# Second half of the output gate computed in two groups of 512 columns, three pair-steps by sums, with the side work placed anew

## The chip, the cores and the metric

The kernel runs on one core of a Trainium2 chip. The metric is the device time of one execution in microseconds, as the median of several runs. A core has five engines that run side by side, each in the order of its own instructions: TensorE (PE, with its weight loads as PEld), VectorE (DVE), ScalarE (ACT), GpSimd (POOL) and SyncE (SP), which here issues most of the DMAs.

## The reference

One layer: a gated linear attention mixer and a squared-ReLU MLP, each with an RMS norm ahead and a residual around it, for 256 tokens of width 2048 in fp32. Only the lines that the change touches in some way:

```python
def _gla_mixer(h, w_in, w_gate_up, b_gate, o_norm, w_out):
    proj = h @ w_in
    q, k, v, r, g_low = jnp.split(proj, [...], axis=-1)      # widths 1024, 1024, 2048, 2048, 16
    ...                                                        # o: the chunked attention, 256 x 2048
    o = o * lax.rsqrt(jnp.mean(o * o, axis=-1, keepdims=True) + EPS) * o_norm
    return (o * jax.nn.silu(r)) @ w_out

h = x
h = h + _gla_mixer(_rmsnorm(h, gla_norm), w_in, w_gate_up, b_gate, o_norm, w_out)
h = h + _sq_relu_mlp(_rmsnorm(h, mlp_norm), w_up, w_down)
return _rmsnorm(h, final_norm)
```

The change is in how the second half of `r` (columns 1024 to 2047 of the gate) is computed, and in what is done beside it.

## The kernel before, in words

**Numbers.** fp32 values are split into a high and a low part of a type that TensorE takes at full rate. A product is three matmuls: high by high, low by high, high by low. Weights arrive by DMA in `raw` tiles (six in turn, with a seventh now and then); ACT casts the high part (`copy_hi`, L123) and DVE subtracts it from the raw tile for the low part (L136). There are five slots for high and low parts. Tokens are two tiles of 128; a matmul has 128 x 128 against 128 x 256.

**Two ways for a group of 512 columns.** `x_group` (L731) calls `group` (L294), which walks over eight pair-steps of 2 x 128 rows of `w_in` in a given order. A plain pair-step is 24 matmuls. A pair-step in the list `summed` is done by sums: the 2 x 2 blocks of weights and of activations are added up such that seven block products do the work of eight, which makes 21 matmuls. Nine of them go at once, on the plain blocks and a block that an accumulating DMA of POOL (L335) has added up; the other twelve are "pending" and stand behind the next step's matmuls, since DVE first has to form the sums of the weights (`weight_sums`, L233 and L234), ACT to cast them and DVE to subtract (L365). At the end of a group with summed steps, `combine` adds up the two banks of sums (ACT copies L735 and L736, DVE L737 to L740), and `put_all` adds the plain banks (L745) and hands each token tile on. For the gate that is `gate_x`: Silu on ACT (L803) and the product with the attention's output `on` on DVE (L804). The function in `between[step]` is run after that step. Four such groups, V0 and V1 for values and G0 and G1 for the gate's first half, precede the place of the change.

**The gate's second half.** It is computed by `natural` (L183): 16 steps of 128 rows and 24 matmuls (L181), over 1024 columns at a time, accumulated in four banks. Rows 5 and 6 (`EVEN`) are inserted at places 3 and 5. After each step `pump` takes functions from the deque `side` and from `jobs`. Behind the third step stand two turns, then four loads of the residual (`load_h`, 0.5 MB each, SP's queue), then `begin_out(0)`, which copies the residual into the banks of the output projection's first group. `jobs` holds two pieces of `make_sums` (L242), which form sums of `w_out` ahead of their use. At the end `gate_out` makes four Silu (L823) and four products with `on` (L824).

**Turns.** `turn(..., q)` transposes the columns of `on` for four blocks of 128 (eight PE transposes, L845) and splits them for use as activations of the output projection; for pair-rows 0, 1, 6 and 7 it forms their block sums too (L834 to L837), for the others it writes plain high and low parts (ACT L858, DVE L859). Turns 0 and 1 need columns 0 to 1023 of `on`, turns 2 and 3 the rest. Turns 2 and 3 stand behind the second step of the output projection's first group, `out_group(0)`, whose order begins with the pair-rows 3 and 0.

**What sets the order.** Each engine runs its instructions in the order of the program that a scheduler arranges, with `issue_after` tying certain casts, subtractions and matmuls to one another. PE is in order throughout: a transpose that waits holds all matmuls behind it.

Of the kernel before, what the change touches and what calls it, by code (L numbers as in the profile page):

```python
# [29 lines left out]
AF = mybir.ActivationFunctionType  # L30
# [17 lines left out]
G = 1024  # L48
# [21 lines left out]
def tile_gla_mlp(ctx, tc, x, xt, cols, w_vg, w_in, w_gate, w_out, w_up, w_down, final_norm, out):  # L70
# [657 lines left out]
        scores(hd)  # L728
        scores(hd + 1, spare)

    def x_group(n, c0, order, summed, between, put, rows_of={}):  # L731

        def combine(p16, p57):
            tt = nc.vector.tensor_tensor
            nc.scalar.copy(comb_x[:, 1::2], two(p16))  # L735
            nc.scalar.copy(comb_x[:, 0::2], two(p57))  # L736
            tt(comb_x[:, 3], comb_x[:, 1], comb_x[:, 3], op=ALU.add)  # L737
            tt(comb_x[:, 0], comb_x[:, 0], comb_x[:, 3], op=ALU.subtract)
            tt(comb_x[:, 3], comb_x[:, 3], comb_x[:, 2], op=ALU.add)
            tt(comb_x[:, 2], comb_x[:, 0], comb_x[:, 2], op=ALU.subtract)  # L740

        def put_all(banks):
            for t in range(NT):
                o = comb_x[:, 2 * t : 2 * t + 2]
                nc.vector.tensor_tensor(o, two(banks[t]), o, op=ALU.add)  # L745
                put(o.rearrange("p f s -> p (f s)"), t)

        def at_of(kp):
            def at(k):
                if k < A12:  # L750
                    return [x_forms[kp][:, i, k] for i in range(2)]
                t, i = divmod((A11, A12, A21, A22).index(k), 2)
                return plain_x(2 * kp + i, t)
            return at

        def row(kt, t):
            return (row_x if (kt, t) in [(2 * kp + i, t) for kp in rows_of for t, i in rows_of[kp][:1]] else plain_x)(kt, t)

        group(
            lambda kp: w_in[2 * kp * P : 2 * (kp + 1) * P, c0 : c0 + GT], [psum_bank(i) for i in x_banks[n % 2]], x_sums,  # L760
            order, summed, between, row, at_of, combine, put_all, filled=False, rows_of=rows_of,
        )

    V0 = (5, 6, 2, 0, 7, 3, 4, 1), (0, 4)
# [41 lines left out]

    x_group(2, 4 * KEYW, *G0, {i + 1: f for i, f in enumerate(attends[:6])}, gate_x(0), {2: FIRST[2]})
    x_group(3, 4 * KEYW + GT, *G1, {i: f for i, f in enumerate(attends[6:])}, gate_x(GT), {2: FIRST[2]})
    acc_free.clear()
    acc_free.extend(x_banks[0] + x_sums + x_banks[1])  # L810
    jobs.extend(next(make))


    oth = otl = None

    some = mid.tile([P, 7, 512], F32, tag="qt", name="some")

    def gate_out(acc, c0):
        for c in range(2):
            for t in range(NT):  # L820
                lo = c0 + 512 * c
                s = some[:, 2 * c + t]
                nc.scalar.activation(s, acc[t][c], AF.Silu, scale=r1[:, t : t + 1])  # L823
                nc.vector.tensor_tensor(on[:, t, lo : lo + 512], on[:, t, lo : lo + 512], s, op=ALU.mult)  # L824

    FORMED = (0, 1, 6, 7)
    raw_forms = [in_forms(some[:, 4:6].rearrange("p a b -> p (a b)")), in_forms(mid.tile([P, G], F32, tag="db", name="form"))]
# [11 lines left out]
    def turn(src, row, gain, q, forms_of=None, banks=None):  # L839

        bs = banks or [aux_bank(), aux_bank()]
        for i in range(4):
            kt, b, o = 4 * q + i, bs[i // 2], i % 2 * T
            for t in range(NT):
                newest[0] = nc.tensor.matmul(  # L845
                    b[:, o + t * P : o + (t + 1) * P], src[:, t, kt * P : (kt + 1) * P], ident, is_transpose=True,
                    start=i % 2 == t == 0, stop=i % 2 == t == 1, skip_group_check=True,
                ).ins
        for kp in (2 * q, 2 * q + 1):
            if forms_of and kp in FORMED:  # L850
                turn_pair(kp, bs[kp - 2 * q], gain, forms_of(kp))
                continue
            for kt in (2 * kp, 2 * kp + 1):
                i = kt - 4 * q
                b, o = bs[i // 2], i % 2 * T
                s = b[:, o : o + T].rearrange("p (t s) -> p t s", t=NT)
                dh, dl = row(kt)
                nc.scalar.activation(dh, s, AF.Copy, scale=gain(kt))  # L858
                nc.vector.scalar_tensor_tensor(dl, s, gain(kt), dh.bitcast(F32), op0=ALU.mult, op1=ALU.subtract)  # L859

    once_x = lambda kt, t: (plain_x if kt == EVEN[1] else row_x)(kt, t)
    oth, otl = (big.tile([P, KT * T + 192], F32R, tag="B", name="ot" + i) for i in "hl")

    of_pairs = big.tile([P, 4 * G + 64], F32R, tag="C", name="of")[:, OFF:-16].rearrange("p (b i f s) -> p b i f s", b=2, i=2, f=8)
# [37 lines left out]
    def spare_out(g):  # L902
        return [psum_bank(out_ids[2 * (1 - g % 2) + t], "aux") for t in range(NT)]

    side.extend([nothing] * 2 + [lambda: (
        turn(on, turned_o, gain_o, 0, forms_o),
        turn(on, turned_o, gain_o, 1, forms_o, [psum_bank(i, "aux") for i in r_banks[4:]]),
    )])
    side.extend([nothing] + [lambda i=i: load_h(i % 2, i // 2) for i in range(4)] + [nothing] * 2 + [lambda: begin_out(0)])
    r_banks = list(acc_free)  # L910
    out_ids = r_banks[4:] + r_banks[:4]
    acc = natural(once_x, rows(w_in, 5 * KEYW), G, HALF, order=even_at(3, 5))
    flush()
    gate_out(acc, G)
    hs = const.tile([P, NT, 4], F32, name="hs")

    GROUPS = D // GT
# [27 lines left out]
    def ssq_h(g):  # L945
# [5 lines left out]
    newest[0] = None  # L951
    ordered[0] = True
    out_group(0, ORDER[0], FORMED, {
        1: lambda: (turn(on, turned_o, gain_o, 2), turn(on, turned_o, gain_o, 3, forms_o, spare_out(0))),
        3: lambda: begin_out(1),
    })
    hth, htl = (big.tile([P, KT, T], F32R, tag="A" + i, name="h" + i, bufs=1) for i in "hl")
# [517 lines left out]
```

## Time and profile before

| | us |
|---|---|
| median of 3 runs | 1040.14 |
| lowest and highest | 1039.99, 1042.02 |
| span of the profiled execution | 1038.7 |
| PE busy in it | 1030.1 (99%) |
| DVE busy | 903.9 (87%) |
| ACT busy | 754.8 (73%) |
| POOL busy | 136.1 (13%) |
| gate's second half on PE (L181) | 238.41 to 283.76 |

The profiled execution's span lies 1.4 us under the median of the runs. Line numbers are those of the kernel before. A row of a timeline joins neighbouring instructions of one form; its time goes from the first start to the last end, so that pitches are read from one start to the next.

### The profile page before, as it was taken

The numbers are of one execution on the slowest core, as the hardware profiler recorded it, in microseconds if no ns is written. First come the engines' busy times: TensorE is split into PE (matmuls) and PEld (weight loads), VectorE is DVE, ScalarE is ACT, GpSimd is POOL, SyncE is SP. The second block draws the span as 40 slices with busy tenths as digits, with TensorE's granted clock in tenths as the row PEclk, the third lists the DMA queues.
The fourth block names the chain that finished last, engine by engine and source line by source line (L and its number), as shares of the span: only waits on it lengthen the run. The fifth ranks groups of instructions, "written<-read, shape, count | busy, mean of one in ns | idle before, by whom it ended". The sixth has DMA issues, their size and how long they took to land.

```text
span 1038.7 us, 23376 instructions
## 1 busy us (share of the span) xinstructions
PE 1030.1 (99%) x9019; PEld 1029.7 (99%) x9019; DVE 903.9 (87%) x1254; ACT 754.8 (73%) x1130; POOL 136.1 (13%) x180
## 2 busy tenths in 40 slices
PE   9999999999999999999999999999999999999997
PEld 9999999999999999999999999999999999999997
DVE  7769768898697866989989999999999999999887
ACT  7775556676586754688779788788778778778685
POOL 0000111310100001111111111111212111111100
PEclk9999999999999999999999999999999999999999
DMA  9967867758877776678888888887887888887772
GB/s 335 332 199 216 262 208 212 209 157 312 252 238 254 249 246 193 191 215 231 232 234 226 231 240 228 236 238 222 245 231 220 244 226 228 244 237 213 229 245 84
DMA packets 128591, 240.04 MB, mean 231 GB/s; under 512 B 11440, under 2 KB 30000, under 8 KB 128352
## 3 DMA queue, kind: packets, MB, share of 16 engines
q1 hardware_dynamic: 107456, 215.32, 64.3%
q0 software_dynamic: 20304, 21.64, 12.3%
q8 instruction: 70, 1.15, 0.4%
q10 hardware_dynamic: 720, 1.60, 0.4%
q14 instruction: 41, 0.34, 0.1%
HBM read 232.22 MB, written 6.29 MB: 230 GB/s over the span
## 4 chain that ended last, share of the span: by engine, by line
PE 99%; issue 0%; ACT 0%; DVE 0%; POOLq 0%; POOL 0%; DVEq 0%
PE up L1023 34%; PE acc L1023 28%; PE acc L305 16%; PE acc L181 10%; PE acc L224 6%; PE aux L224 2%; PE aux L181 1%; PE aux L845 1%; PE aux L696 1%; PE aux L399 0%; ACT sqf L1362 0%; PE acc L595 0%; DVE hf L1434 0%; POOLq L1471 0%; POOL rf L521 0%
## 5 line engine op out<-in xcount | busy, mean ns | idle before, releaser
L123 ACT CAST hi<-raw 128x1024 fp32r<-128x1024 f32 (+4 forms) x654 | 518.6, 822 | 200.0 <-DVE raw L233 64.2
L136 DVE TENSOR_TENSOR lo<-raw,hi 128x768 fp32r<-128x768 f32 (+4 forms) x228 | 233.6, 1032 | 56.6 <-ACT hi L123 50.9
L1023 PE MATMUL acc<-hi,act 128*128 128x256 f32 x1696 | 247.7, 276 | 0.0
L1023 PE MATMUL up<-hh,hi 128*128 128x256 f32 x1024 | 238.7, 276 | 0.0
L1023 PE MATMUL up<-hl,hi 128*128 128x256 f32 x1024 | 238.7, 276 | 0.0
L1023 PEld LDWEIGHTS acc<-hi,act 128*128 128x128 f32 x1696 | 217.6, 188 | 0.0
L170 DVE TENSOR_TENSOR lo<-raw,hi 128x1024 fp32r<-128x1024 f32 x160 | 194.4, 1218 | 22.8 <-ACT hi L123 21.3
L1023 PEld LDWEIGHTS up<-hl,hi 128*128 128x128 f32 x1024 | 192.3, 188 | 0.0
L1023 PEld LDWEIGHTS up<-hh,hi 128*128 128x128 f32 x1024 | 192.3, 188 | 0.0
L1233 POOL DMA_DIRECT2D raw<-in_w_down x112 | 97.1, 867 | 518.6 <-DMA raw<-in_w_down 258.3
L1293 DVE TENSOR_TENSOR lo<-raw,hi 128x1024 fp32r<-128x1024 f32 x112 | 136.3, 1217 | 1.1 <-ACT hi L123 1.1
L1023 PE MATMUL up<-hh,lo 128*128 128x256 f32 x1024 | 137.0, 276 | 0.0
L1023 PE MATMUL acc<-lo,act 128*128 128x256 f32 x848 | 133.9, 276 | 0.0
L1023 PEld LDWEIGHTS up<-hh,lo 128*128 128x128 f32 x1024 | 125.7, 188 | 0.0
L1023 PEld LDWEIGHTS acc<-lo,act 128*128 128x128 f32 x848 | 113.4, 188 | 0.0
L234 DVE TENSOR_TENSOR raw<-raw 128x512 f32<-128x512 f32 x137 | 94.5, 689 | 3.4
L233 DVE TENSOR_TENSOR raw<-raw 128x256 f32<-128x256 f32 x137 | 57.8, 422 | 9.3 <-DMA raw<-in_w_out 6.4
L181 PE MATMUL acc<-hi,xA 128*128 128x256 f32 (+1 forms) x376 | 55.8, 281 | 0.0
L181 PEld LDWEIGHTS acc<-hi,xA 128*128 128x128 f32 x376 | 49.6, 189 | 0.1
L224 PE MATMUL acc<-xA,hi 128*128 128x256 f32 x288 | 49.2, 276 | 0.0
L224 PEld LDWEIGHTS acc<-xA,hi 128*128 128x128 f32 x288 | 43.3, 188 | 0.0
L1150 ACT COPY sums<-acc 128x512 f32<-128x512 f32 x46 | 26.8, 583 | 22.6 <-PE acc L1023 22.5
(226 smaller groups left out, 1443.7 us busy)
## 6 DMA issues: line engine op xcount, KB each, us to landing
raw<-in_w_up SPq DMA_DIRECT2D x128, 512.0 KB, 4.4
raw<-in_w_down SPq DMA_DIRECT2D x224, 256.0 KB, 4.3
raw<-in_w_in SPq DMA_DIRECT2D x69, 512.0 KB, 4.7
raw<-in_w_down POOLq DMA_DIRECT2D x112, 128.0 KB, 5.1
raw<-in_w_out SPq DMA_DIRECT2D x22, 512.0 KB, 6.1
raw<-in_w_down SPq DMA_DIRECT2D x16, 512.0 KB, 4.9
raw<-in_w_vg SPq DMA_DIRECT2D x14, 520.0 KB, 8.7
raw<-in_w_out SPq DMA_DIRECT2D x24, 256.0 KB, 5.3
```

The costliest lines, as they stand in the source:

```text
L123: last_hi[0] = nc.scalar.copy(to, raw)
L136: last_lo[0] = nc.vector.tensor_tensor(lo[:, s], raw[:, s], hi[:, s].bitcast(F32), op=ALU.subtract)
L170: last_lo[0] = nc.vector.tensor_tensor(to[1], dst, to[0].bitcast(F32), op=ALU.subtract)
L181: newest[0] = nc.tensor.matmul(o[:, m], x, w[:, m], start=first and c == 0, stop=last, skip_group_check=True).ins
L224: nc.tensor.matmul(o, u[:, i, s], m, start=kt == 0 and n == 0 and j % 2 == 0, stop=kt == KT - 1 and n == 2, skip_group_check=True,)
L233: nc.vector.tensor_tensor(u[:, 2], u[:, 0], u[:, 2], op=ALU.subtract)
L234: return nc.vector.tensor_tensor(u[:, 1::2], u[:, 1::2], u[:, 2:3].to_broadcast([P, 2, T]), op=ALU.subtract)
L305: newest[0] = nc.tensor.matmul(bank[:, o + d : o + d + T], x, w[:, d : d + T], start=(not filled or bank in sums_banks) and bank.name not ...
L1023: newest[0] = nc.tensor.matmul(o, x, w, start=first, stop=last, skip_group_check=True).ins
L1150: last_end[0] = nc.scalar.copy(to, src).ins
L1233: nc.gpsimd.dma_start(out=raw[:, :T], in_=src[:, 0, T:], accum_op=ALU.add)
L1293: last_lo[0] = nc.vector.tensor_tensor(to[1][:, :G], u, to[0][:, :G].bitcast(F32), op=ALU.subtract)
```

## The change

`x_group` gets an argument `plain_put`, which replaces `put_all` for a group without summed steps. `natural`, `gate_out`, `even_at`'s order and the deque's entries for this stage go. In their place stand two more groups:

- `x_group(4, ...)`: 512 columns, pair-rows in the order 5, 0, 2, 4, 3, 1, 6, 7 with 0, 4 and 1 by sums; turns 0 and 1 behind the second step; `gate_x(G)` at the end.
- `x_group(5, ...)`: the last 512 columns, order 0, 1, 5, 2, 4, 3, 6, 7, none by sums; the loads of the residual behind steps 0, 1 and 3, turn 2 behind step 2, the two jobs of `make_sums` behind steps 4 and 5, with `begin_out(0)`; `gate_plain` at the end, two Silu and two products.

Turn 3 alone stays behind the second step of `out_group(0)`, and takes its banks from the auxiliary ones.

```diff
--- before.py
+++ after.py
@@ -728,7 +728,7 @@
         scores(hd)
         scores(hd + 1, spare)
 
-    def x_group(n, c0, order, summed, between, put, rows_of={}):
+    def x_group(n, c0, order, summed, between, put, rows_of={}, plain_put=None):
 
         def combine(p16, p57):
             tt = nc.vector.tensor_tensor
@@ -758,7 +758,7 @@
 
         group(
             lambda kp: w_in[2 * kp * P : 2 * (kp + 1) * P, c0 : c0 + GT], [psum_bank(i) for i in x_banks[n % 2]], x_sums,
-            order, summed, between, row, at_of, combine, put_all, filled=False, rows_of=rows_of,
+            order, summed, between, row, at_of, combine, plain_put or put_all, filled=False, rows_of=rows_of,
         )
 
     V0 = (5, 6, 2, 0, 7, 3, 4, 1), (0, 4)
@@ -806,22 +806,19 @@
 
     x_group(2, 4 * KEYW, *G0, {i + 1: f for i, f in enumerate(attends[:6])}, gate_x(0), {2: FIRST[2]})
     x_group(3, 4 * KEYW + GT, *G1, {i: f for i, f in enumerate(attends[6:])}, gate_x(GT), {2: FIRST[2]})
-    acc_free.clear()
-    acc_free.extend(x_banks[0] + x_sums + x_banks[1])
-    jobs.extend(next(make))
-
+    now = next(make)
 
     oth = otl = None
 
     some = mid.tile([P, 7, 512], F32, tag="qt", name="some")
 
-    def gate_out(acc, c0):
-        for c in range(2):
+    def gate_plain(c0):
+        def put(banks):
             for t in range(NT):
-                lo = c0 + 512 * c
-                s = some[:, 2 * c + t]
-                nc.scalar.activation(s, acc[t][c], AF.Silu, scale=r1[:, t : t + 1])
-                nc.vector.tensor_tensor(on[:, t, lo : lo + 512], on[:, t, lo : lo + 512], s, op=ALU.mult)
+                s = some[:, t]
+                nc.scalar.activation(s, banks[t], AF.Silu, scale=r1[:, t : t + 1])
+                nc.vector.tensor_tensor(on[:, t, c0 : c0 + GT], on[:, t, c0 : c0 + GT], s, op=ALU.mult)
+        return put
 
     FORMED = (0, 1, 6, 7)
     raw_forms = [in_forms(some[:, 4:6].rearrange("p a b -> p (a b)")), in_forms(mid.tile([P, G], F32, tag="db", name="form"))]
@@ -858,7 +855,6 @@
                 nc.scalar.activation(dh, s, AF.Copy, scale=gain(kt))
                 nc.vector.scalar_tensor_tensor(dl, s, gain(kt), dh.bitcast(F32), op0=ALU.mult, op1=ALU.subtract)
 
-    once_x = lambda kt, t: (plain_x if kt == EVEN[1] else row_x)(kt, t)
     oth, otl = (big.tile([P, KT * T + 192], F32R, tag="B", name="ot" + i) for i in "hl")
 
     of_pairs = big.tile([P, 4 * G + 64], F32R, tag="C", name="of")[:, OFF:-16].rearrange("p (b i f s) -> p b i f s", b=2, i=2, f=8)
@@ -902,16 +898,22 @@
     def spare_out(g):
         return [psum_bank(out_ids[2 * (1 - g % 2) + t], "aux") for t in range(NT)]
 
-    side.extend([nothing] * 2 + [lambda: (
-        turn(on, turned_o, gain_o, 0, forms_o),
-        turn(on, turned_o, gain_o, 1, forms_o, [psum_bank(i, "aux") for i in r_banks[4:]]),
-    )])
-    side.extend([nothing] + [lambda i=i: load_h(i % 2, i // 2) for i in range(4)] + [nothing] * 2 + [lambda: begin_out(0)])
-    r_banks = list(acc_free)
-    out_ids = r_banks[4:] + r_banks[:4]
-    acc = natural(once_x, rows(w_in, 5 * KEYW), G, HALF, order=even_at(3, 5))
-    flush()
-    gate_out(acc, G)
+    out_ids = x_banks[0] + x_banks[1] + x_sums
+    two_turns = lambda q, ids: (
+        turn(on, turned_o, gain_o, q, forms_o),
+        turn(on, turned_o, gain_o, q + 1, forms_o, [psum_bank(i, "aux") for i in ids]),
+    )
+    G2 = (5, 0, 2, 4, 3, 1, 6, 7), (0, 4, 1)
+    G3 = (0, 1, 5, 2, 4, 3, 6, 7), ()
+    x_group(4, 5 * KEYW, *G2, {1: lambda: two_turns(0, x_banks[1])}, gate_x(G), {2: FIRST[2]})
+    x_group(5, 5 * KEYW + GT, *G3, {
+        **{i: lambda i=i: load_h(i % 2, i // 2) for i in (0, 1)},
+        2: lambda: turn(on, turned_o, gain_o, 2),
+        3: lambda: (load_h(0, 1), load_h(1, 1)),
+        4: lambda: now[10](), 5: lambda: (now[11](), begin_out(0)),
+    }, None, {2: FIRST[2]}, gate_plain(G + GT))
+    acc_free.clear()
+    acc_free.extend(out_ids)
     hs = const.tile([P, NT, 4], F32, name="hs")
 
     GROUPS = D // GT
@@ -951,7 +953,7 @@
     newest[0] = None
     ordered[0] = True
     out_group(0, ORDER[0], FORMED, {
-        1: lambda: (turn(on, turned_o, gain_o, 2), turn(on, turned_o, gain_o, 3, forms_o, spare_out(0))),
+        1: lambda: turn(on, turned_o, gain_o, 3, forms_o),
         3: lambda: begin_out(1),
     })
     hth, htl = (big.tile([P, KT, T], F32R, tag="A" + i, name="h" + i, bufs=1) for i in "hl")
```

**PE, first turn.** In the fences, `acc` is an accumulation bank, `xA`, `xE` and `xe_gt` are plain activations, `xf` activations' block sums, `hi` and `lo` weight parts; `on` with `ident` is a transpose. PE before, around the first turns, in the third step of the gate's second half and the fourth:

```order
L181 MATMUL acc<-lo,xA 128x256 x4
L181 MATMUL acc<-hi,xA 128x256 x8
L181 MATMUL acc<-lo,xA 128x256 x4
L181 MATMUL acc<-hi,xA 128x256 x4
L845 MATMUL aux<-ident,on 128x128 x16
L181 MATMUL acc<-hi,xe_gt 128x256 x4
L181 MATMUL acc<-lo,xe_gt 128x256 x4
L181 MATMUL acc<-hi,xe_gt 128x256 x4
```

PE after, around the same turns, in the second step of the new group and the third:

```order
L305 MATMUL acc<-lo,xA 128x256 x2
L305 MATMUL acc<-hi,xA 128x256 x4
L305 MATMUL acc<-hi,xf 128x256 x2
L305 MATMUL acc<-lo,xA 128x256 x2
L305 MATMUL acc<-lo,xf 128x256
L842 MATMUL aux<-ident,on 128x128 x16
L305 MATMUL acc<-hi,xe_gt 128x256 x4
L305 MATMUL acc<-lo,xe_gt 128x256 x2
```

The first step's 24 matmuls are ahead of these rows. The turns' transposes stand behind 33 matmuls of the new group in place of 72, and six rather than twelve matmuls on `xe_gt` follow.

**DVE, the seam between the gate's halves.** `comb` are the sums being combined, `on` the attention's output. DVE before, from the combine of group 3 to its last product and the first sums of a turn:

```order
L737 TENSOR_TENSOR comb<-comb 128x256
L738 TENSOR_TENSOR comb<-comb 128x256
L739 TENSOR_TENSOR comb<-comb 128x256
L740 TENSOR_TENSOR comb<-comb 128x256
L136 TENSOR_TENSOR lo<-raw,hi 128x1024
L745 TENSOR_TENSOR comb<-acc,comb 128x512 x2
L136 TENSOR_TENSOR lo<-raw,hi 128x1024
L804 TENSOR_TENSOR on<-on,comb 128x512 x2
L136 TENSOR_TENSOR lo<-raw,hi 128x1024 x2
L835 TENSOR_TENSOR some<-some 128x128
```

DVE after, the same stretch:

```order
L737 TENSOR_TENSOR comb<-comb 128x256
L738 TENSOR_TENSOR comb<-comb 128x256
L365 TENSOR_TENSOR lo<-raw,hi 128x1024
L739 TENSOR_TENSOR comb<-comb 128x256
L136 TENSOR_TENSOR lo<-raw,hi 128x768
L740 TENSOR_TENSOR comb<-comb 128x256
L233 TENSOR_TENSOR raw<-raw 128x256
L745 TENSOR_TENSOR comb<-acc,comb 128x512 x2
L234 TENSOR_TENSOR raw<-raw 128x2x256
L136 TENSOR_TENSOR lo<-raw,hi 128x1024
L804 TENSOR_TENSOR on<-on,comb 128x512 x2
L832 TENSOR_TENSOR some<-some 128x128
```

Between the combine and the product L804 stand now a low part of sums (L365), a low part of 768 columns and the sums of weights (L233, L234) of the new group's first summed step, with a low part of 1024 columns; the turn's sums follow the product at once.

**PE, behind the stage.** PE after, in the first two steps of the output projection (`oth`, `otl` are turned activations, `of` their block sums):

```order
L305 MATMUL acc<-hi,oth 128x256 x2
L305 MATMUL acc<-hi,otl 128x256 x2
L305 MATMUL acc<-lo,oth 128x256 x2
L305 MATMUL acc<-hi,of 128x256 x6
L305 MATMUL acc<-lo,of 128x256 x3
L842 MATMUL aux<-ident,on 128x128 x8
L305 MATMUL acc<-hi,oth 128x256 x2
```

PE before, at the same place:

```order
L305 MATMUL acc<-hi,oth 128x256 x2
L305 MATMUL acc<-hi,otl 128x256 x2
L305 MATMUL acc<-lo,oth 128x256 x2
L305 MATMUL acc<-hi,of 128x256 x6
L305 MATMUL acc<-lo,of 128x256 x3
L845 MATMUL aux<-ident,on 128x128 x16
L305 MATMUL acc<-hi,oth 128x256 x2
```

One turn of eight transposes stands there in place of two.

## Rows read from the trace of the kernel before

**Rows 1.** The head of the page: span; busy time of each engine; the chain by engine.

```profile
span 1038.7 us, 23376 instructions
...
PE 1030.1 (99%) x9019; PEld 1029.7 (99%) x9019; DVE 903.9 (87%) x1254; ACT 754.8 (73%) x1130; POOL 136.1 (13%) x180
...
PE 99%; issue 0%; ACT 0%; DVE 0%; POOLq 0%; POOL 0%; DVEq 0%
```

**Rows 2.** Pieces of the chain that ended last, in order of time: start us, us, what.

```profile
148.51 8.12 PE acc L305 x69
...
221.57 17.00 PE acc L305 x150
238.57 8.17 PE acc L181 x72
248.49 35.43 PE acc L181 x312
...
289.41 23.25 PE acc L305 x201
```

**Rows 3.** Busy time (count) of each engine by stretch; then clock, DMA share, GB/s.

```profile
239.00:284.00 45.00, 45.00 (x400) 45.00 (x399) 31.44 (x41) 25.49 (x35) 4.63 (x6) 1.00 0.81 275
...
302.00:312.00 10.00, 10.00 (x87) 10.00 (x86) 10.00 (x16) 7.81 (x12) 0.86 (x1) 1.00 0.98 282
240.00:246.00 6.00, 6.00 (x55) 6.00 (x54) 5.21 (x7) 3.34 (x4) 0.00 (x0) 1.00 1.03 404
...
1031.00:1033.00 2.00, 0.14 (x2) 0.00 (x0) 1.53 (x8) 0.77 (x3) 0.55 (x1) 1.00 0.94 355
...
1036.00:1038.00 2.00, 0.00 (x0) 0.00 (x0) 0.00 (x0) 0.00 (x0) 0.00 (x0) 0.52 0.31 117
```

**Rows 4.** Timeline of PE: start us, us, engine, line, operation, out<-in, tile, count.

```profile
188.46 0.64 PE L305 MATMUL acc<-hi,xe_gt 128*128 128x256 f32 x4
...
238.41 0.62 PE L181 MATMUL acc<-hi,xA 128*128 128x256 f32 x4
...
246.57 1.91 PE L845 MATMUL aux<-ident,on 128*128 128x128 f32 x16
248.24 0.72 PE L181 MATMUL acc<-hi,xe_gt 128*128 128x256 f32 x4
...
283.76 0.39 PE L305 MATMUL acc<-hi,oth 128*128 128x256 f32 x2
...
287.50 1.91 PE L845 MATMUL aux<-ident,on 128*128 128x128 f32 x16
```

**Rows 5.** Timeline of DVE where the value groups end and the gate begins.

```profile
189.39 0.42 DVE L737 TENSOR_TENSOR comb<-comb 128x256 f32<-128x256 f32 x1
...
192.11 0.96 DVE L136 TENSOR_TENSOR lo<-raw,hi 128x768 fp32r<-128x768 f32 x1 [0.15 <-ACT hi L123]
...
197.32 0.74 DVE L559 SCALAR_TENSOR_TENSOR vl<-comb,r,vh 128x512 fp32r<-128x512 f32 x1
```

**Rows 6.** Timeline of DVE at both ends of the gate's second half.

```profile
237.71 0.42 DVE L737 TENSOR_TENSOR comb<-comb 128x256 f32<-128x256 f32 x1
...
243.56 1.29 DVE L804 TENSOR_TENSOR on<-on,comb 128x512 f32<-128x512 f32 x2
...
283.60 2.49 DVE L824 TENSOR_TENSOR on<-on,some 128x512 f32<-128x512 f32 x4
```

**Rows 7.** Timeline of ACT where the gate's second half begins; idle time before in brackets.

```profile
236.39 0.58 ACT L735 COPY comb<-acc 128x512 f32<-128x512 f32 x1
...
238.38 1.05 ACT L123 CAST hi<-raw 128x1024 fp32r<-128x1024 f32 x1 [0.93 <-PE acc L305]
```

**Rows 8.** Groups by line and form, DVE: count, busy us, mean ns, idle before.

```profile
L234 DVE TENSOR_TENSOR raw<-raw 128x512 f32<-128x512 f32 x137 | 94.5, 689 | 3.4
...
L233 DVE TENSOR_TENSOR raw<-raw 128x256 f32<-128x256 f32 x137 | 57.8, 422 | 9.3 <-DMA raw<-in_w_out 6.4
...
L365 DVE TENSOR_TENSOR lo<-raw,hi 128x1024 fp32r<-128x1024 f32 x21 | 25.6, 1219 | 4.0 <-ACT hi L123 3.3 <-PE acc L305 0.7
```


## The prediction

> **What bounds the kernel now.** The head of the page comes first: TensorE (PE) is busy 99% of a span of 1038.7 us, and the chain of work that ended last is 99% PE [rows 1]. So a change pays only by what it takes from, or adds to, PE's stream. The pieces of that chain, in order of time, then give the pitch at which PE takes a 128x256 matmul: 17.00 us for 150 of them, 0.1133 us, in the group ahead of the gate's second half, and 8.17 for 72, 0.1135, in the gate's second half itself. Two other pieces are slower: 8.12 for 69 (0.1177) and 23.25 for 201 (0.1157) [rows 2]. Last, the table by stretch says what stands in the gate's second half: PE busy for all 45 us, VectorE (DVE) 31.4, ScalarE (ACT) 25.5, DMA at a share of 0.81 and the clock at 1.00. In 302:312, in the first group of the output projection, DVE is busy for all 10 us [rows 3]. PE has no idle time to win here; what it has to lose is a wait that the new order could bring.
>
> **Matmuls taken out.** The gate's second half has 16 steps of 24 matmuls, 384. After, 13 pair-steps have 24 and three have 21, which makes 375. Nine matmuls by 0.1133 [rows 2] are **-1.02 us**, all on PE and so all on the path. Transposes stay at 16 + 8 + 8.
>
> **A wait for turn 1.** This is the term I find largest. Turns 0 and 1 transpose columns 0 to 1023 of `on`, and turn 1 needs the product L804 of group 3, the group just before. Before, PE started its gate steps at 238.41 and came to the transposes at 246.57, behind 72 matmuls [rows 4]. After, only 24 + 9 = 33 matmuls stand ahead: 238.41 + 33 x 0.1133 = 242.15. The 16 transposes take 248.24 - 246.57 = 1.67 [rows 4], so turn 1 begins at 242.15 + 0.84 = 242.99, and its second transpose, the first to read the other token tile, at about 243.1.
>
> When is L804 done? Before, at 243.56 + 1.29 = 244.85 [rows 6], 1.7 before PE came. After, DVE has more ahead of it, since groups 3 and 4 now join as two by-sums groups do. That sequence (L737, L738, the sums' low part L365, L739, a 768-wide low part, L740, L233, two L745, L234, a 1024-wide low part, then the two last operations) has run once in the trace, where the value groups end and the gate begins. There the 768-wide low part began 2.72 us after L737 (192.11 against 189.39), and the last operation ended at 197.32 + 0.74 = 198.06, 5.95 us after that low part's start [rows 5]. Its last two operations were two of 0.74; ours are two in 1.29 [rows 6], so 5.95 - 1.48 + 1.29 = 5.76. The 768-wide low part cannot start before its cast. ACT's cast at this place had to wait for PE to free its buffer and started at 238.38, 1.05 for 1024 columns [rows 7]; for 768, three quarters, I estimate 0.8, so 239.2 at the earliest. At the latest I take L737 where it stands now, 237.71 [rows 6], plus 2.72: 240.4. Now L737 is held by L735, which ACT begins at 236.39 [rows 7] behind two 1024-wide casts; after, one of those casts stands behind it, so I take a place nearer the early end, 239.6. Then L804 ends at 239.6 + 5.76 = 245.4 and PE waits 245.4 - 243.1, rounded to **+2.2 us** since the first transposes overlap. The ends are 239.2, a wait of 1.8, and 240.4, a wait of 3.0. As a floor, L804 no earlier than today (244.85) is 1.7. All of PE's stream is behind that transpose, in order, so the wait is on the path in full.
>
> **The slow piece in the output projection.** The 201 matmuls from 289.41 took 23.25 us; at 0.1133 they would take 22.77, so 0.48 is lost there [rows 2], most of it in 302:312 where DVE has no pause [rows 3]. The change takes turn 2 and half of the four L824 products (2.49 us together [rows 6]) out of DVE's work ahead of that stretch. I take it that DVE then keeps up, and that the stretch keeps the usual pitch: **-0.4 us**. The bounds are -0.48 and 0; that it gets worse I exclude, since DVE only loses work there.
>
> **What is hidden.** A by-sums step costs DVE 0.96 + 0.42 + 0.69 + 1.22 = 3.29 where a plain one costs 1.22 [rows 5, 8]: three are 6.2 more. The one combine of group 4 is four of 0.42 [rows 5], and its put two more additions, about the 1.3 of two L804 [rows 6]: some 9 in all. DVE was busy 31.4 of 45 [rows 3], so about 41 of 45: covered, with little left, and if the cover goes, PE waits for a low part. The h loads are four DMAs on SP's queue, moved among the second group's weight loads; they are needed only by begin_out at that group's sixth step. With them and POOL's three more accumulating loads (0.13 MB each, by the tile's size) the two groups load some 10.9 MB in 45 us, 240 GB/s, where 404 were reached in 240:246 [rows 3]; an accumulating load that is late delays only its own step's sums, which PE reads a step later. The two `make_sums` jobs at steps 4 and 5 of the second group keep their work and have no reader there. Turn 2 is due 72 x 0.1133 = 8.2 us after the second group's start. Its product is ready 245.4 - 238.41 = 7.0 after the start by the same sequence, but the seam's own order lets DVE go to L804 sooner: slack 1.2 or more. Turn 3 comes 33 matmuls, 3.74 us, after the second group's end, as it does now (287.50 against 283.76 [rows 4]). Now the four products end at 283.60 + 2.49 = 286.09 [rows 6], 1.4 ahead; after, there are two rather than four, with one cast and one copy more in front, and I count about 1 us of slack. All of these are 0.
>
> **Sum.** -1.02 + 2.2 - 0.4 = +0.8: the span goes from 1038.7 to 1039.5. The median of the runs is 1040.14, 1.4 above the profiled span; I leave that as it is, so **1040.9 us**. With the ends of the wait and of the slow piece this case reaches from -1.02 + 1.7 - 0.48 = +0.2 to -1.02 + 3.0 = +2.0, 1040.3 to 1042.1. A measurement of this kernel can tell about 0.2% (2.1 us) from no change, so this counts as the same.
>
> **Rivals.**
> *No wait.* The products are ready in time: -1.02 - 0.4, **1038.7**. For it: DVE could serve L804 before the low parts. Against: the order puts three low parts and two sums of weights ahead of it, and even today's end, 244.85, is too late. This is also where the change would do what a count of matmuls promises. Chance 0.08, the same side.
> *DVE late at the seam (slower).* At the seam of values and gate the last operation ended 198.06 - 188.46 = 9.60 after the start of the new group [rows 4, 5]. With that here, L804 ends at 248.0 and the wait is 4.9, 2.7 more: **1043.6**. It decides from an end 8.2 us after the start (246.6), when the wait passes 3.5. For it: the sequence is the same. Against: L737 stood 0.93 after the seam there and stands 0.70 before it here [rows 4 to 6]. Chance 0.12.
> *A slow pitch that stays (slower).* 69 matmuls ran at 0.1177 after a run of scores that six matmuls on a single k-row (`xe_gt`) followed, without recovering; behind the 16 transposes of the gate stand 12 such matmuls, and the 312 from 248.49 took 35.43, 0.1136 [rows 2]. After the change six stand there. If the pitch stays at 0.1177, it does so for 150 + 192 + 33 = 375 matmuls, 0.0044 each, 1.65 us: **1042.6**. For it: the short run behind the scores. Against: what came ahead there were scores, and behind transposes the pitch came back. Chance 0.12.
> *The clock falls.* The granted clock was 1.00 throughout 239:284, transposes included. At the end of the program it still read 1.00 in 1031:1033 with PE busy 0.14 of 2 us, and 0.52 in 1036:1038, with PE idle [rows 3]. A stretch at the lower of its two levels, 1.2 rather than 2.4 GHz, as long as that last row would cost 1.0 us: 1041.9. Chance 0.04, on the same side. The Trainium skill, "TensorE: Matmul & The Clock Gate", sections "HAM oscillation — how this bites in real kernels" and "Part 4: PE-mode transpose", says that a wait between bursts of matmuls sends the clock back so that the next burst starts at half rate, and that transposes do not count as busy time in the same way. By that rule, a wait between two batches of transposes is the worst place for one. The rows agree that an idle PE ends at the lower level, and show none that is reached inside the kernel.
>
> **Chances.** Forecast 0.60, no wait 0.08, clock 0.04: the same within 0.2%, 0.72. Late seam 0.12 and slow pitch 0.12: slower, 0.24. A gain over 0.2% needs 1.1 us beyond everything counted, and no row holds it: 0.04. The range takes in the forecast with its ends, no wait, the clock and the slow pitch, and leaves out the late seam and the large gain: 1038.6 to 1042.8.
>
> **What would show it.** On PE's rows, an idle time of some 2 us inside the transposes about 33 matmuls into the gate's second half, released by L804 on DVE; none means the first rival, over 3.5 the second. The pitch of the 150 matmuls after it: 0.1133 or 0.1177. In the first output group, about 0.1135 in the 200 matmuls behind turn 3, rather than 0.1157. Idle PE at turn 2, turn 3 or a low part in groups 4 and 5 would show that a cover I counted on was missing; a granted clock under 1.00 near the wait would show the clock.

## The result: slower by 0.5%

The changed kernel takes 1045.54 us (median of five runs, 1044.92 to 1047.29) against 1040.4 for the kernel before: a ratio of 1.005, 95% interval 1.004 to 1.0061, some 4 to 6 us more. The forecast was 1040.9, no change that can be measured, with a range up to 1042.8. Lines of the changed kernel are two to four off those of before: a turn's transposes are L842, its sums L832 and L834, the residual's copies L896; the second group's Silu and products with `on` are L819 and L820.

The head of the page, span, busy time and the chain by engine, answers to [rows 1]:

```profile
span 1042.8 us, 23411 instructions
...
PE 1029.6 (99%) x9010; PEld 1028.1 (99%) x9010; DVE 911.3 (87%) x1269; ACT 757.8 (73%) x1138; POOL 136.9 (13%) x183
...
PE 95%; DVE 1%; DMA 1%; issue 1%; ACT 0%; POOL 0%; POOLq 0%; DVEq 0%; ACTq 0%; SPq 0%
```

PE ran nine instructions less, as counted, and has lost its hold on the chain: some 5% of it now goes through DVE, DMA and the others. What PE waits for, from 230 to 300 us (total, times, longest), has three entries, where the kernel before has none:

```profile
PE aux L842 <- DVE on L820: 2.0, 2, 1.4
PE aux L842 <- DVE on L804: 1.8, 1, 1.8
PE acc L305 <- DVE lo L136: 0.4, 1, 0.4
```

Their places, in PE's timeline (idle time ahead of a row in brackets):

```profile
241.79 1.04 PE L842 MATMUL aux<-ident,on 128*128 128x128 f32 x8
...
244.59 1.38 PE L842 MATMUL aux<-ident,on 128*128 128x128 f32 x8 [1.76 <-DVE on L804]
...
282.80 0.62 PE L305 MATMUL acc<-hi,xE 128*128 128x256 f32 x4
283.80 0.50 PE L305 MATMUL acc<-lo,xE 128*128 128x256 f32 x2 [0.38 <-DVE lo L136]
284.14 0.63 PE L305 MATMUL acc<-hi,xE 128*128 128x256 f32 x4
...
289.79 0.52 PE L305 MATMUL acc<-lo,of 128*128 128x256 f32 x3
290.92 0.41 PE L842 MATMUL aux<-ident,on 128*128 128x128 f32 x2 [0.61 <-DVE on L820]
292.76 0.88 PE L842 MATMUL aux<-ident,on 128*128 128x128 f32 x6 [1.43 <-DVE on L820]
293.39 0.48 PE L305 MATMUL acc<-hi,oth 128*128 128x256 f32 x2
```

The first wait, 1.76 us, is turn 1, waiting for L804 as forecast. The second, 0.38, is a matmul at the end of the second group. The third and fourth, 0.61 and 1.43, are turn 3, where I had counted 1 us to spare. A wait costs somewhat more than its idle time: from one start to the next, 244.59 - 241.79 = 2.80 for eight transposes that otherwise take 0.84, which is 1.96 more for 1.76 idle.

### The profile page after: what moved, and what is told of

It reads as the page before. It is cut to its first block, busy times and chain, and to the rows that moved or that the text cites. A ratio compares the mean times of both kernels' runs of the same rounds, so it can differ in the third digit from the quotient of the medians.

```text
span 1042.8 us, 23411 instructions
## 1 busy us (share of the span) xinstructions
PE 1029.6 (99%) x9010; PEld 1028.1 (99%) x9010; DVE 911.3 (87%) x1269; ACT 757.8 (73%) x1138; POOL 136.9 (13%) x183
## 3 DMA queue, kind: packets, MB, share of 16 engines
q8 instruction: 70, 1.15, 0.4%
## 4 chain that ended last, share of the span: by engine, by line
PE 95%; DVE 1%; DMA 1%; issue 1%; ACT 0%; POOL 0%; POOLq 0%; DVEq 0%; ACTq 0%; SPq 0%
PE up L1025 33%; PE acc L1025 28%; PE acc L305 18%; PE acc L224 6%; PE acc L181 6%; PE aux L224 2%; PE aux L181 1%; DMA made<-hi 1%; DMA raw<-in_w_out 1%; DVE lo L136 1%; PE aux L696 1%; PE aux L842 1%; PE aux L399 0%; ACT sqf L1364 0%; DVE on L820 0%
## 5 line engine op out<-in xcount | busy, mean ns | idle before, releaser
L234 DVE TENSOR_TENSOR raw<-raw 128x512 f32<-128x512 f32 x140 | 96.6, 690 | 3.4
L233 DVE TENSOR_TENSOR raw<-raw 128x256 f32<-128x256 f32 x140 | 59.2, 423 | 8.2 <-DMA raw<-in_w_out 5.2
L305 PE MATMUL acc<-hi,xA 128*128 128x256 f32 x408 | 64.2, 276 | 0.0
L305 PEld LDWEIGHTS acc<-hi,xA 128*128 128x128 f32 x408 | 54.6, 188 | 0.0
```

Source lines behind the costliest of these rows:

```text
L233: nc.vector.tensor_tensor(u[:, 2], u[:, 0], u[:, 2], op=ALU.subtract)
L234: return nc.vector.tensor_tensor(u[:, 1::2], u[:, 1::2], u[:, 2:3].to_broadcast([P, 2, T]), op=ALU.subtract)
L305: newest[0] = nc.tensor.matmul(bank[:, o + d : o + d + T], x, w[:, d : d + T], start=(not filled or bank in sums_banks) and bank.name not ...
```

## Where ACT and DVE stood still

The pieces of the chain between group 4 and the output projection name what lies behind the waits (start us, us, what):

```profile
221.21 17.01 PE acc L305 x150
...
245.97 14.33 PE acc L305 x126
...
265.77 6.85 DMA raw<-in_w_out
...
272.67 0.65 POOL raw L335
273.32 7.96 DMA made<-hi
...
293.63 22.86 PE acc L305 x201
...
317.37 20.82 PE acc L305 x183
```

From 265.77 to 281.28 the chain runs over a load of `w_out`, an accumulating load that POOL issues for it (L335), and the store of a `make_sums` job (`made<-hi`). The timelines of POOL, ACT and DVE in the same stretch:

```profile
272.67 0.85 POOL L335 DMA_DIRECT2D raw<-in_w_out  x1 [33.03 <-DMA raw<-in_w_out]
273.32 0.75 POOL L256 DMA_DIRECT2D made<-hi  x1
```

```profile
268.51 1.05 ACT L255 CAST hi<-raw 128x1024 fp32r<-128x1024 f32 x1 [0.79 <-PE acc L305]
...
272.40 0.83 ACT L855 ACTIVATE oth<-aux,colt 128x256 fp32r<-128x256 f32 x2
281.43 2.00 ACT L123 CAST hi<-raw 128x1024 fp32r<-128x1024 f32 x2 [8.20 <-DMA made<-hi]
```

```profile
273.95 0.87 DVE L856 SCALAR_TENSOR_TENSOR otl<-aux,colt,oth 128x256 fp32r<-128x256 f32 x2
282.51 1.23 DVE L136 TENSOR_TENSOR lo<-raw,hi 128x1024 fp32r<-128x1024 f32 x1 [7.69 <-ACT hi L123]
```

The job's cast L255 was done at 269.56. Its store, L256, is the next instruction on POOL after L335, and L335 had to wait for the plain loads of its tile until 272.67. So the store went out 3.8 us after its data were ready and took 8 more to land. It reads from one of the five buffers for high parts; the cast that is next to use that buffer stood still for 8.2 us, with everything behind it on ACT, and DVE stood still for 7.7. PE lived on what was ready until 283.42, waited for a low part, and then found ACT and DVE with a backlog: both Silu and both products of the second group came late for turn 3.

In the kernel before, the order on POOL is the other way round, as its second trace (run e12) shows; its store had no accumulating load ahead of it:

```profile
262.09 0.61 POOL L256 DMA_DIRECT2D made<-hi  x1 [36.45 <-ACT hi L255]
265.95 0.55 POOL L260 DMA_DIRECT2D made<-lo  x1 [3.26 <-DVE lo L259]
270.76 0.88 POOL L335 DMA_DIRECT2D raw<-in_w_out  x1 [4.26 <-issue]
```

## Experiments

All but e12 are the changed kernel with one or a few lines different; e7 to e11 and e13 build on e1. Steps are counted from 0, as in the code, and `...` marks what is cut from an edit.

**e1: the jobs earlier.** They run behind steps 1 and 2 of the second group.

```diff
-        **{i: lambda i=i: load_h(i % 2, i // 2) for i in (0, 1)},
-        2: lambda: turn(on, turned_o, gain_o, 2),
+        0: lambda: load_h(0, 0), 1: lambda: (load_h(1, 0), now[10]()),
+        2: lambda: (turn(on, turned_o, gain_o, 2), now[11]()),
...
-        4: lambda: now[10](), 5: lambda: (now[11](), begin_out(0)),
+        5: lambda: begin_out(0),
```

> The two make_sums jobs run behind steps 1 and 2 of the second group instead of 4 and 5, so that their two stores stand ahead of the first accumulating load of w_out on POOL's queue. Theory (the store L256 stands behind that load, keeps a high-part slot, and ACT's cast waits 8.2 us for it): ACT's wait on the store falls under 1 us, PE's wait for a low part (0.65 with restart) and the waits of turn 3 (2.4) go, 3.0 us less than 1045.5, about 1042.5. Rival 1 (the second group's DMAs are too many, h loads among them): the job's load and stores now lie among the h loads, the wait stays, 1045 to 1046. Rival 2 (turn 3 stands only 33 matmuls behind the seam and its product's own chain is too long): only the 0.65 goes, about 1044.9, and turn 3 still waits 2 us.

1042.5 us (1041.61 to 1045.94), as the first theory has it. The store goes out at once (264.09 on POOL, 0.4 behind its cast), and only turn 1 still waits on PE. ACT still waits for the store, 3.6 us where I had expected under 1: the store took 7.1 us to land although no load stood ahead of it. Nobody follows closely at that place (PE's waits from 230 to 320, ACT's from 255 to 300):

```profile
PE aux L842 <- DVE on L804: 1.8, 1, 1.8
```

```profile
ACT hi L123 <- DMA made<-hi: 3.6, 1, 3.6
```

Turn 3 no longer waits: its transposes start at 290.18 and the second L820 ends at 289.34, 0.8 us earlier. The slack that I had counted is there when DVE is not held up.

**e4: the same jobs, the store from ACT's queue.** This leaves the amount and the place of the work alone and takes only POOL's queue out of it.

```diff
-            nc.gpsimd.dma_start(out=made[key][0], in_=to[0][:, :G].bitcast(F32))
+            (nc.scalar if key[1:] == (3, 6) else nc.gpsimd).dma_start(out=made[key][0], in_=to[0][:, :G].bitcast(F32))
```

> Jobs stay at steps 4 and 5, but the high part's store is issued by ACT, right behind its cast, and no longer by POOL behind the accumulating load. Theory: the store is issued near 269.6 instead of 273.3 and lands some 3.7 us sooner, so ACT's wait falls from 8.2 to about 4.5, the backlog behind it goes and with it most of the 3.0 us: 1042.5 to 1043.5. Rival 1 (DMAs crowded): the store takes as long as the crowd lasts, 1045 or more. Rival 2 (distance of turn 3): about 1044.9.

1042.29 us (1041.83 to 1042.74). The same gain by the other way. The edit changes two things, the time of issue (270.23 instead of 273.32) and the queue. The timeline of ACT:

```profile
269.15 1.05 ACT L255 CAST hi<-raw 128x1024 fp32r<-128x1024 f32 x1 [0.79 <-PE acc L305]
...
270.23 0.34 ACTq L256 DMA_DIRECT2D made<-hi  x1
...
275.86 2.00 ACT L123 CAST hi<-raw 128x1024 fp32r<-128x1024 f32 x2 [1.99 <-DVE otl L856]
```

The cast that waited 8.2 us now waits 2.0, where I had expected 4.5. The profile names DVE's L856 for it, but that was done at 275.46, while the store takes 5.6 us to land, up to 275.8, just ahead of the cast at 275.86. So it is probably still the store that the cast waits for.

**e6: the residual's loads out of the second group.** They stand behind steps 2 to 5 of the first.

```diff
-x_group(4, ..., {1: lambda: two_turns(0, x_banks[1])}, ...)
+x_group(4, ..., {1: lambda: two_turns(0, x_banks[1]), 2: lambda: load_h(0, 0), 3: lambda: load_h(1, 0), 4: lambda: load_h(0, 1), 5: lambda: load_h(1, 1)}, ...)
-        **{i: lambda i=i: load_h(i % 2, i // 2) for i in (0, 1)},
-        3: lambda: (load_h(0, 1), load_h(1, 1)),
```

> The four h loads move out of the second group, behind steps 2 to 5 of the first. Theory (POOL's queue order): the store still stands behind the accumulating load, which still waits for its two plain loads; ACT still waits 5 us or more for the store, and the time stays within 1 us of 1045.5. Rival 1 (crowded DMAs): the store takes half the time, ACT's wait falls under 3 us and 3.0 us go, 1042.5. Rival 2: 1044.9.

1045.58 us (1044.87 to 1047.71): nothing changed. ACT still waits for the store, and turn 3 for its products:

```profile
ACT hi L123 <- DMA made<-hi: 7.9, 1, 7.9
```

```profile
PE aux L842 <- DVE on L820: 2.0, 2, 1.4
```

So it is the queue, and not the load on the DMA engines from the residual. With e1 and e4, the cause of 3 of the 5 us is shown: a store that stands behind an accumulating load on POOL's queue. How much of it is the late issue (3.8 us) and how much the slow landing (8 us) is not parted.

**e2: turns 0 and 1 one step later.**

```diff
-x_group(4, 5 * KEYW, *G2, {1: lambda: two_turns(0, x_banks[1])}, ...)
+x_group(4, 5 * KEYW, *G2, {2: lambda: two_turns(0, x_banks[1])}, ...)
```

> Turns 0 and 1 stand behind the third step of the first new group instead of the second, 69 matmuls in instead of 33. My prediction's term (turn 1 waits 2.2 us for L804, in order, on the path): the wait goes and the time falls by 2.2 to about 1043.3, with the second group's waits as they are. Rival: the seam is bound by DVE, which is busy 21 of 22 us there, so that the wait only moves to a low part or a sum later in the group: 1045 to 1045.5.

1042.57 us (1041.54 to 1044.09), 3.0 less rather than 2.2. Turn 1 no longer waits, but turn 2 does, since DVE is now behind at the seam of the two groups. And the matmuls behind the turns of the first group run at a slower pitch, 18.86 us for 160, 0.1179 (PE's waits; a piece of the chain):

```profile
PE aux L842 <- DVE on L804: 1.3, 2, 1.1
```

```profile
248.67 18.86 PE acc L305 x160
```

Against these two losses stands a gain that I had not foreseen: the order on POOL has turned round with the edit, and the store goes out ahead of the accumulating load, with the job at the same step (POOL's timeline):

```profile
267.73 0.57 POOL L256 DMA_DIRECT2D made<-hi  x1 [27.50 <-ACT hi L255]
271.79 0.85 POOL L335 DMA_DIRECT2D raw<-in_w_out  x1 [3.49 <-DVE on L804]
```

The waits for a low part and of turn 3 are gone with it: a third way to the same 3 us. With turn 1's 2.2, less the idle 1.3 at turn 2 with its restart, and 0.7 for the pitch (18.86 against 160 x 0.1133 = 18.13), that makes the 3.0.

**e8: jobs early, and every turn later.** Turns 0 and 1 behind step 3, turn 2 behind step 4, and a step that begins with matmuls on `xe_gt` behind each.

```diff
-x_group(4, 5 * KEYW, *G2, {1: lambda: two_turns(0, x_banks[1])}, gate_x(G), {2: FIRST[2]})
+x_group(4, 5 * KEYW, *G2, {3: lambda: two_turns(0, x_banks[1])}, gate_x(G), FIRST)
-        2: lambda: (turn(on, turned_o, gain_o, 2), now[11]()),
+        2: lambda: now[11](),
+        4: lambda: turn(on, turned_o, gain_o, 2),
...
```

> The kernel e1_jobs_early with turns 0 and 1 two steps later, 78 matmuls into the first new group, and turn 2 two steps later in the second; the step behind each turn begins with the matmuls on xe_gt, which stand behind the turns in every kernel but e2. Theory A (the slow pitch of e2, 160 matmuls at 0.1179, came from the missing xe_gt matmuls behind the turn): the pitch is 0.1133 again, turn 1's 2.2 us go, and nothing takes their place: 1042.5 - 2.2 = 1040.3, the same as before. Theory B (it came from DVE, busy all the time there): the pitch stays near 0.118 for some 100 matmuls, 0.5 us, 1040.8 or more. Rival C (DVE is too full): PE waits for a low part or for turn 2, 1041.5 or more.

1040.57 us (1039.19 to 1042.13), ratio 0.9998, interval 0.9989 to 1.0007: the loss is gone, and so is any gain. The pitch behind the turns is the usual one although DVE is busy 12.91 of 13 us there (249 to 262; busy time and count of PE, PEld, DVE, ACT, POOL; then clock, DMA share, GB/s), so a full DVE is not enough to bring the slow pitch (117 matmuls in these 13 us, against 113 in e2). Turn 3 waits, a loss that I had not expected: ahead of its products, DVE's sum of weights L233 had stood still for 4.4 us, for a load of `w_out`. The stretch of 249 to 262, then the wait:

```profile
249.00:262.00 13.00, 13.00 (x117) 13.00 (x116) 12.91 (x24) 9.42 (x17) 0.00 (x0) 1.00 0.85 266
```

```profile
PE aux L842 <- DVE on L820: 1.1, 1, 1.1
```

**e9: by-sums steps later in the first group.** Jobs early, order 5, 6, 0, 2, 4, 3, 1, 7, turns 0 and 1 behind step 2, turn 2 behind step 3.

```diff
-    G2 = (5, 0, 2, 4, 3, 1, 6, 7), (0, 4, 1)
-    G3 = (0, 1, 5, 2, 4, 3, 6, 7), ()
+    G2 = (5, 6, 0, 2, 4, 3, 1, 7), (0, 4, 1)
+    G3 = (0, 1, 5, 4, 2, 3, 6, 7), ()
...
```

> As e1_jobs_early, but the first new group takes pair-rows 5, 6, 0, 2, 4, 3, 1, 7, so that the first by-sums step is the third and turns 0 and 1 stand 57 matmuls in; turn 2 is one step later, behind a group order with pair-row 2 one place later. Theory: L804 is ready about 6.5 us behind the seam and the second turn's transposes come 57 x 0.1133 + 0.94 = 7.4 us behind it, so no wait at turn 1, 1040.3. The last by-sums step stands one place nearer the end, so combine ends later: if turn 2 waits for its product the time is 1041 or more.

1044.4 us (1043.51 to 1047.43): a miss. Turn 1 has no wait, but turn 3 has 2.2, and a pitch of 17.45 us for 148 matmuls, 0.1179, began behind the turns although the `xe_gt` matmuls stood there. So their absence is not what makes the slow pitch either. In this execution (1047.43 us) the clock fell behind turn 3's wait:

```profile
PE aux L842 <- DVE on L820: 2.2, 2, 1.4
```

```profile
291.00:293.00 2.00, 0.43 (x3) 0.22 (x3) 1.97 (x4) 1.97 (x3) 0.00 (x0) 0.95 1.06 287
293.00:294.00 1.00, 1.00 (x5) 1.00 (x6) 1.00 (x2) 1.00 (x3) 0.00 (x0) 0.50 0.50 182
294.00:296.00 2.00, 2.00 (x11) 2.00 (x10) 2.00 (x4) 1.65 (x5) 0.00 (x0) 0.50 0.20 54
```

**e10 and e13: two and three by-sums steps without waits.** Jobs early; in the order 5, 6, 4, 2, 0, 3, 1, 7 pair-rows 4 and 0 go by sums (e10), in 5, 6, 4, 2, 0, 1, 3, 7 also 1 (e13); turns as in e9.

```diff
-    G2 = (5, 6, 0, 2, 4, 3, 1, 7), (0, 4, 1)
+    G2 = (5, 6, 4, 2, 0, 3, 1, 7), (4, 0)          # e10
+    G2 = (5, 6, 4, 2, 0, 1, 3, 7), (4, 0, 1)       # e13
```

> As e9_sums_later, with two by-sums steps (4 and 0) instead of three in the order 5, 6, 4, 2, 0, 3, 1, 7: three matmuls more, 0.34 us, and 2.1 us less of DVE's work. If DVE's load is what takes the gain away, this is faster than e9 in spite of the matmuls (under 1040.3); if not, it is 0.3 slower, 1040.6.

> The kernel e10_two_sums with the third by-sums step back, pair-row 1 behind pair-row 0: order 5, 6, 4, 2, 0, 1, 3, 7. Three matmuls less: 1040.0 - 0.3 = 1039.7 if DVE keeps up. Rival: two by-sums steps in a row hold DVE 3.3 us each against 2.4 on PE, so that turn 2 or a low part waits: 1040.5 or more.

e10 takes 1040.04 us (1039.01 to 1046.69), ratio 1.0 (0.9987 to 1.0013), e13 1040.49 (1040.08 to 1042.2), ratio 0.9999 (0.999 to 1.0008). Neither beats the kernel before by what can be measured. The span of e10's trace, 1037.5, is 1.2 under that of [rows 1], and its list of PE waits is empty from 230 to 320. The third by-sums step brought nothing more, the time that the rival has. Its wait is small: turn 3's eight transposes take 1.15 us from start to start (288.05 to 289.20) where e10's take 0.80, and that is what three matmuls are worth.

**e7: turn 2 back in the output projection.** On top of e1.

```diff
-        2: lambda: (turn(on, turned_o, gain_o, 2), now[11]()),
+        2: lambda: now[11](),
-        1: lambda: turn(on, turned_o, gain_o, 3, forms_o),
+        1: lambda: (turn(on, turned_o, gain_o, 2), turn(on, turned_o, gain_o, 3, forms_o, spare_out(0))),
```

> The kernel e1_jobs_early with turn 2 put back beside turn 3 into the output projection's first group. Prediction's term (turn 2's work on DVE starts the slow piece there): the 201 matmuls behind the turns take 23.2 us again instead of 22.86, and the time is about 0.3 us above e1, 1042.8. Rival (the slow piece had another cause, such as the h loads or the products L824): they take 22.86 and the time stays at 1042.5, less 0.1 for one batch of transposes less.

**e12: the kernel before, a second trace.**

> The kernel before, unchanged, for a second trace. If the slow piece behind turn 3 (201 matmuls in 23.25 us) belongs to this program, it is there again, 23.2; if it comes and goes from one execution to the next, the 201 matmuls take 22.86, as in e1, e2, e7, e8 and e10, or the slow stretch lies elsewhere.

The 201 matmuls behind turn 3, pieces of the chain of e7 and of e12:

```profile
294.44 22.86 PE acc L305 x201
```

```profile
289.41 23.26 PE acc L305 x201
```

e12 (1040.59 us, 1040.08 to 1041.09) repeats the slow piece of [rows 2] (23.25) to within a hundredth, so it belongs to that program. e7 has turn 2's work on DVE at the same place as before and does not have it. Nor does the changed kernel, although its DVE is just as full there (9.88 of 10 us in 306:316). My cause for it has fallen; what starts it is open. e7 takes 1042.4 us (1041.36 to 1045.76), the same as e1 within its spread.

The execution of e7 that was profiled (1045.76 us) shows what the change risks on top. Turn 1 waits 1.8 us, as in e1 and the changed kernel (1.9 in e4), but here the clock falls:

```profile
245.00:246.00 1.00, 0.41 (x2) 0.20 (x2) 1.00 (x3) 1.00 (x4) 0.00 (x0) 1.00 0.18 18
246.00:248.00 2.00, 1.92 (x9) 1.92 (x10) 2.00 (x6) 1.31 (x3) 0.00 (x0) 0.51 0.78 253
248.00:249.00 1.00, 1.00 (x7) 1.00 (x6) 1.00 (x4) 0.61 (x2) 0.00 (x0) 0.50 0.09 10
...
252.00:290.00 38.00, 38.00 (x325) 38.00 (x324) 28.86 (x35) 21.90 (x27) 4.59 (x6) 1.00 0.89 286
```

In 246 to 249, 1.2 GHz is granted instead of 2.4, and 3 us of matmuls take twice their time; behind it the slow pitch stands up to turn 3 (one piece of the chain, with the end of the low stretch in it, has 375 matmuls in 45.07 us, 0.1202).

**e11: turns 0 and 1 one step earlier**, on top of e1, to lengthen the wait.

```diff
-    G2 = (5, 0, 2, 4, 3, 1, 6, 7), (0, 4, 1)
+    G2 = (5, 2, 0, 4, 3, 1, 6, 7), (0, 4, 1)
-x_group(4, ..., {1: lambda: two_turns(0, x_banks[1])}, ...)
+x_group(4, ..., {0: lambda: two_turns(0, x_banks[1])}, ...)
```

> The kernel e1_jobs_early with turns 0 and 1 one step earlier, 24 matmuls into the first new group instead of 33, and pair-row 2 right behind them. Turn 1's wait is 33 - 24 = 9 matmuls, 1.0 us, longer, about 3.2 with its restart. If only the wait counts, the time is 1042.5 + 1.0 = 1043.5 and the clock reads 1.00 behind the wait. If a wait of this length can bring the clock to its lower level, as the traces of e7 and e9 show behind waits of some 2 us (0.50 and 0.51 granted, matmuls at 0.213 for 3 us), the profile shows 0.5 behind the transposes, and the time is 1.5 us or more above that: 1045 or more.

1049.52 us (1048.82 to 1051.47). I had the wait's length wrong: not 3.2 but 7.7 us, since in this order DVE meets a weight sum that waits 2.6 us for an accumulating load ahead of the combine. The clock fell during it and stood at its lower level behind it:

```profile
PE aux L842 <- DVE on L804: 7.7, 2, 7.2
```

```profile
242.00:245.00 3.00, 1.05 (x10) 0.81 (x8) 2.15 (x5) 1.08 (x2) 0.86 (x1) 1.00 0.73 227
245.00:246.00 1.00, 0.00 (x0) 0.00 (x0) 1.00 (x2) 1.00 (x3) 0.00 (x0) 0.68 0.44 67
...
250.00:252.00 2.00, 1.25 (x5) 0.88 (x6) 1.76 (x6) 0.35 (x1) 0.00 (x0) 0.50 0.89 248
```

## Why the prediction was wrong, point by point

- **Matmuls, -1.02: right.** 9010 instructions on PE instead of 9019, and the new group runs at the usual pitch (126 matmuls in 14.33 us behind the turns, 0.1137).
- **Turn 1, +2.2: right, with its mechanism.** L804 was to end 7.0 us behind the seam; the new group starts at 238.05 and the pair of products ends at 245.05. From start to start the eight transposes of turn 0 take 2.80 instead of 0.84, and those of turn 1 1.14 instead of 0.83 (244.59 to 245.73, the next matmul): 2.3 us.
- **Slow piece, -0.4: right in size, wrong in cause.** 22.86 instead of 23.25. I took it that DVE, with less work ahead, keeps up; but e7 has turn 2 back there and 22.86 still, and DVE in the changed kernel is as full as before. That the size came out is luck.
- **What is hidden, 0: wrong; this is the step that failed.** The sentence was that the two `make_sums` jobs "keep their work and have no reader there". Nobody reads the sums there, but the store holds a buffer that the next casts need, and it stands on a queue. I weighed SP's queue and the accumulating loads of the two groups, and did not look at which of POOL's instructions the moved store now stands behind. The price: 0.7 us for the low part (282.80 to 284.14 is 1.34 for six matmuls that take 0.68), and 2.4 for turn 3 (289.79 to 293.39 is 3.60 for three matmuls and eight transposes, 0.34 + 0.84). e1 and e4 give 3.0 and 3.2 back.
- **Turn 3's slack of about 1 us: right only without the stall.** It is 0.8 in e1, and cannot pay for 8 us of standstill. In e8 and e9 it is gone for another reason: DVE's sum of weights ahead of the products stood still for 4.4 and 4.0 us, for a load of `w_out`. Whether turn 2's later place brings that about is not shown.
- **Sum.** -1.0 - 0.4 + 2.3 + 0.7 + 2.4 = +4.0 by the trace. The stage ends at 317.37 instead of 313.53 and began 0.36 earlier (221.21 instead of 221.57): 4.2. The 0.2 that is left is a slow pitch behind the wait for the low part: the 48 matmuls from 284.14 to 289.79 take 5.65 us, 0.1177 each. The medians differ by 5.1. Of the 0.9 beyond the stage, 0.6 is that the profiled execution was the fastest of the five, whose spans are 1042.8, 1043.4, 1043.4, 1043.5 and 1045.2 us. The median one has the same mean granted clock as the profiled one, 0.998, so a fallen clock does not explain this 0.6, which stays open; the two longest have 0.996. Some 0.3 more lies outside the span: a run's time is 2.1 us above its span here, and 1.7 to 1.8 in e12.
- **The clock, rival with 0.04: too low.** It was 1.00 in this trace, and fell in e7 and e9 behind waits of the same length (1.8 and 1.4 us), in e11 within one of 7 us. In e1 the four runs with a mean granted clock of 0.998 took 1041.6 to 1042.5 us, the three with 0.996 took 1044.1 to 1045.9. The Trainium skill, "TensorE: Matmul & The Clock Gate", section "HAM oscillation — how this bites in real kernels", has the rule, a pause between bursts of matmuls that sends the clock back. These traces agree, and add that here a wait of 1.4 to 1.8 us does it in one execution and not in another (e7 and e9 against the changed kernel and e1). A fall took some 3 us at the lower level in e7 and e9, and in e11, where PE stood idle for half of it, some 10.
- **Late seam and slow pitch, 0.12 each:** the seam came as forecast, not late. Behind the turns the slow pitch did not come in this kernel, but in e2, e7 and e9; here it came for the 48 matmuls behind the wait for a low part. Neither `xe_gt` matmuls behind the turns (e9 has them) nor a full DVE (e8 has one) decide it. What does is open.

## What to carry to other kernels

Of a step that is moved, list for each queue what its DMAs will stand behind: a store that reads from a shared buffer behind a load that waits holds the buffer for both times, and the engine that uses the buffer next stops with all its work. Where an engine is busy throughout, a wait costs its own length, its restart, and now and then a clock that falls behind it; here the loss was five times what nine matmuls are worth, and turn 1's wait and the store's queue made up most of it. Once these two were gone (e8, e10, e13), the gain from fewer matmuls was too small to measure.

## What I had not expected of the hardware

The time that the 0.5 MB store L256 takes to land differs widely: 7.96 us in the changed kernel and 7.84 in e6, behind the load on POOL's queue; 7.1 in e1, with no load ahead; 5.1 in e2 and 4.8 in the kernel before; 5.6 from ACT's queue in e4. So the load ahead is not enough to tell it. In the two slowest, the job's other store went out within 0.6 us behind it; whether that matters is not shown.

TensorE's pitch for one and the same matmul has two steady values here, 0.1133 and 0.1179, and either can last for 150 matmuls and more. In the changed kernel the slower one began behind a wait of PE; in the kernel before it began inside the 201 matmuls with no wait near it.
